# An encoder trunk on eight cores: convolutions moved up in the tail of the convolution layer, norm factors kept in PSUM, MLP roots set apart, half-precision sums moved to GpSimd

## The chip, the cores and the metric

The kernel runs on the eight cores of one Trainium2 chip, two sequences of the batch on each core; no core talks to another. The metric is the device time in microseconds (us) of the slowest core. Cores 0 to 3 form one die, 4 to 7 the other. In some executions the cores of one die, or of both, show a lower granted TensorE clock and the time is some per cent longer (in the profiled run of before die 1 had 0.815 and 5282.6 us, die 0 0.992 and 4483.3); those runs are called slow and are not compared with fast ones.

Engines: PE is TensorE, DVE is VectorE, ACT is ScalarE, POOL is GpSimd, SP is SyncE, which here only issues DMAs. In the lines of the profile nearly all work appears under the line of a helper: L334 is the matmul, L348 the activation, L351 an operation on two tensors, L355 tensor with scalar, L359 scalar-tensor-tensor, L366 a copy or cast, L372 a DMA. `arena` is the one large SBUF tile and `ps` is PSUM.

Because runs disturbed by the clock are frequent, I use two more numbers beside the official ratio. The first is the mean span of all *undisturbed cores* of a kernel: cores whose granted clock in that run was at least 0.9905, over all its runs. The second is the time of each *part* (a mixer layer or an MLP) in the profiled run, from its first matmul to the first matmul of the next part, as the mean of those undisturbed cores whose trace has all 22,320 matmuls.

## The reference, cut to what matters

Batch 16, 2048 positions, 1024 channels, four layers; each layer is a mixer and an MLP, both on an RMS-normed input and added to the residual.

```python
def conv_module(h, w_in, dw, dw_bias, ln_g, ln_b, w_out):
    val, gate = jnp.split(h @ w_in, 2, axis=-1)
    v = val * jax.nn.sigmoid(gate)
    v = depthwise_conv(v, dw, width=31, centred) + dw_bias      # shortened
    vn = (v - mean(v)) * lax.rsqrt(var(v) + LN_EPS) * ln_g + ln_b
    return jax.nn.silu(vn) @ w_out

def sq_relu_mlp(h, w_up, w_down):
    a = jax.nn.relu(h @ w_up)
    return (a * a) @ w_down

mixers = (pool, conv, fourier, pool)      # layers 0..3
for i in range(4):
    x = x + mixers[i](rms_norm(x, norm_mix[i]))
    x = x + sq_relu_mlp(rms_norm(x, norm_mlp[i]), mlp_up[i], mlp_down[i])
return rms_norm(x, final_norm)
```

## The kernel before

Each core keeps the residual of one sequence, and cuts it into four tiles `j` of 512 positions and eight chunks `c` of 128 channels. The large products use a seven-product (Strassen-like) scheme, so "H sums" and "weight sums" are additions that must be made ahead of the MLP's matmuls.

In the convolution layer, `glu(c, j)` makes v, which is written to HBM and read again in four shifted copies (`vread`); `conv(k)` convolves one chunk of one tile on TensorE, in the order of tiles 0, 1, 3, 2. For tiles 3 and 2 the sums for the LayerNorm are made by TensorE too (`flush`), into the two banks S1 and S2.

```python
def vread(k):                       # reread, one per 32 rows; ... cut
    for sh in range(4):
        self.dma("sp", ..., vslot(k)[32 * sh:32 * sh + 32], src, reads=toks)

def conv(k):
    c, j = order[k]                                   # tiles 0, 1, 3, 2
    for m in range(8):
        for q in range(4):
            self.mm(bank[32 * q:32 * q + 32, :], dg(c)[:, q * 8 + m, :], v[:, q, m:m + TT], m == 0, m == 7, skip=True)
    # ... result to C with its bias; sq = its square; cb = a bf16 copy (VectorE)
    if j > 1:
        self.copy(cb, C)
        flush(keep=1)
        late.append((j, c, cb, sq))

def flush(only=None, keep=0):
    while len(late) > keep and (only is None or late[0][0] == only):
        _, c, cb, sq = late.pop(0)
        self.mm(S1, self.cm("ones", 128), cb, c == 0, c == DC - 1)
        self.mm(S2, self.cm("ones", 128), sq, c == 0, c == DC - 1)

def ln_stats(j):                    # two reads of the banks on ScalarE, then Ln and Exp
    ...
    self.act(msq, b1, AF.Square)
    self.copy(m, b1, eng="act")
    self.tt(r, b2, msq, ALU.subtract)
    self.act(r, r, AF.Ln, ...); self.act(r, r, AF.Exp, scale=-0.5)

def ln(j, c, lag=2):                # subtract; two steps later multiply, then SiLU on ScalarE
    self.tt(C, C, M[slot[j]], ALU.subtract, eng="pool" if c % 2 or j == 2 else "dve")
    ...

# the tail
for c in range(DC):
    glu(c, 3)
    if c < 4:
        out(0, 2 * c); out(0, 2 * c + 1)
    else:
        self.sq_flush()
    if c > 0:
        conv(7 + c)
    # ...
conv(15)
for c in range(DC):
    conv(16 + c)                    # tile 3
    ln_stats(1) if c == 0 else ln(1, c - 1)
for c in range(DC):
    conv(24 + c)                    # tile 2
    # ... end of LN(1), ln_stats(3) at c == 1, then ln(3, c - 2)
    if c % 2:
        out(1, c // 2)
# ... out(1, 4..7) with ln(3); out(3, 0..7) with ln(2) and the first H sums; out(2, 0..7) with the other H sums
```

`out(j, oc)` is one chunk of the output projection of tile j; it needs all eight SiLU results of that tile. After `out(2, ·)` the MLP begins; it needs the H sums and the weight sums.

In the middle of each MLP two reciprocal roots (`hs[0]`, `hs[1]`: a matmul with ones, then Ln and Exp on ScalarE) stand 0.1 unit apart in the schedule. In the Fourier tail the pieces of H multiply x with a factor that lies in SBUF (`self.RS`).

## Time and profile before

The three runs took 4494.46 to 4496.15 us. The profiled execution had die 1 slow, so I read die 0, and of it core 1. From the list of cores (core, span, granted clock):

```profile
core 1: 4482.6 us, clock 0.992
core 4: 5283.5 us, clock 0.816
```

TensorE is busy 97% of the span. What can be won is the time in which it waits. This is the view of waits of TensorE in core 1: the engine and line that waited, the engine or DMA it waited for, then us in total, times, longest.

```profile
PE ps L334 <- ACT arena L348: 48.4, 51, 2.5
PE ps L334 <- DVE arena L351: 33.9, 27, 3.3
PE ps L334 <- DMA arena<-l_pool_w_in: 16.0, 3, 13.2
PE ps L334 <- DMA arena<-scr_mlp: 5.0, 2, 3.0
PE ps L334 <- ACT ps L348: 4.6, 7, 1.2
PE ps L334 <- DMA arena<-scr_v: 1.7, 2, 1.4
PE ps L334 <- DVE arena L366: 1.6, 4, 1.0
```

Much of it stands in the tail of the two convolution layers. The timeline of core 1 (start, length, engine, line, operation, tiles, shapes, count, and in brackets the idle time before and what ended it) shows the first chunk of out(3) of sequence 0, which goes one matmul at a time because each SiLU comes late:

```profile
773.20 0.38 PE L334 MATMUL ps<-arena 128*128 128x512 bf16 x1 [1.24 <-ACT arena L348]
...
775.28 0.38 PE L334 MATMUL ps<-arena 128*128 128x512 bf16 x1 [0.99 <-ACT arena L348]
776.95 3.22 PE L334 MATMUL ps<-arena 128*128 128x512 bf16 x8 [1.29 <-ACT arena L348]
```

A longer wait can cost more than itself. This is the wait at out(0) in this layer:

```profile
660.29 11.98 PE L334 MATMUL ps<-arena 128*128 128x512 bf16 x58 [2.47 <-ACT arena L348]
```

The granted clock in this trace (the PEclk column of a view of windows) is 0.50 from 660.22 to 663.63.

In the Fourier tail VectorE is the busy engine (35.64 of the 37.00 us from 1300 to 1337 in core 1). These are two stretches of its pieces of H in the timeline of core 1, one before and one while GpSimd adds:

```profile
1304.67 1.41 DVE L359 SCALAR_TENSOR_TENSOR arena<-arena 128x512 bf16<-128x512 f32 x2
1307.73 8.97 DVE L359 SCALAR_TENSOR_TENSOR arena<-arena 128x512 bf16<-128x512 f32 x8
1309.96 4.64 POOL L351 TENSOR_TENSOR arena<-arena 128x512 bf16<-128x512 bf16 x3 [39.30 <-DVE arena L359]
1319.30 3.14 PE L334 MATMUL ps<-arena 128*128 128x512 bf16 x7 [2.44 <-DVE arena L351]
```

Alone, two pieces take 1.41 us; of the next eight, the last four overlap GpSimd and take 1.64 us each, and TensorE waits 2.44 us at the even outputs behind them.

### The profile page before, as it was taken

The numbers are of one execution on the slowest core, as the hardware profiler recorded it, in microseconds if no ns is written. First come the engines' busy times: TensorE is split into PE (matmuls) and PEld (weight loads), VectorE is DVE, ScalarE is ACT, GpSimd is POOL, SyncE is SP. The second block draws the span as 40 slices with busy tenths as digits, with TensorE's granted clock in tenths as the row PEclk, the third lists the DMA queues.
The fourth block names the chain that finished last, engine by engine and source line by source line (L and its number), as shares of the span: only waits on it lengthen the run. The fifth ranks groups of instructions, "written<-read, shape, count | busy, mean of one in ns | idle before, by whom it ended". The sixth has DMA issues, their size and how long they took to land.

```text
span 5291.8 us, 67459 instructions; the slowest of 8 cores (4481.3 to 5291.8 us)
## 1 busy us (share of the span) xinstructions
PE 5210.3 (98%) x22320; PEld 2167.1 (41%) x22320; DVE 2788.4 (53%) x5056; ACT 2048.3 (39%) x3452; POOL 162.2 (3%) x211
## 2 busy tenths in 40 slices
PE   7999999999999999999999999999999999999998
PEld 3444433444444444444444444334444444444443
DVE  3675545665666742666535545354545645425544
ACT  4333435343434434433443334353433333343333
POOL 0000001000010000000000000010000000000000
PEclk9888887888888888888888888888888888888887
DMA  6355634455535552355822334343333133312342
GB/s 142 92 141 168 152 85 103 115 147 157 168 80 141 158 158 77 81 142 173 223 96 98 126 126 115 88 119 112 126 126 122 70 126 126 128 45 98 126 152 107
DMA packets 122742, 652.33 MB, mean 123 GB/s; under 512 B 14624, under 2 KB 55712, under 8 KB 75552
## 3 DMA queue, kind: packets, MB, share of 16 engines
q1 hardware_dynamic: 102240, 517.46, 27.5%
q0 software_dynamic: 20160, 130.56, 13.8%
q8 instruction: 185, 3.03, 0.2%
q14 instruction: 157, 1.29, 0.1%
HBM read 625.35 MB, written 151.07 MB: 147 GB/s over the span
## 4 chain that ended last, share of the span: by engine, by line
PE 95%; DVE 2%; ACT 1%; issue 1%; DMA 1%; POOL 0%; DVEq 0%; SPq 0%; ACTq 0%; POOLq 0%
PE ps L334 95%; DVE arena L351 1%; ACT arena L348 1%; DVE arena L359 1%; DMA arena<-l_pool_w_in 0%; DMA arena<-xT 0%; POOL arena L372 0%; ACT ps L348 0%; DVEq L285 0%; SPq L372 0%; ACT L348 0%; ACTq L285 0%; DVEq L1848 0%; DVE arena L355 0%; SPq L285 0%
## 5 line engine op out<-in xcount | busy, mean ns | idle before, releaser
L334 PE MATMUL ps<-arena 128*128 128x512 bf16 (+4 forms) x22320 | 5210.3, 423 | 63.5 <-ACT arena L348 28.9
L334 PEld LDWEIGHTS ps<-arena 128*128 128x128 bf16 (+1 forms) x22320 | 2167.1, 108 | 3106.1 <-issue 3002.1
L351 DVE TENSOR_TENSOR arena<-arena,ps 128x512 f32<-128x512 f32 (+2 forms) x1026 | 724.1, 718 | 1189.8 <-PE ps L334 1186.4
L351 DVE TENSOR_TENSOR arena<-arena 128x512 bf16<-128x512 bf16 (+4 forms) x2318 | 1105.9, 495 | 182.1 <-ACT arena L348 143.9
L348 ACT ACTIVATE arena<-arena 128x512 bf16<-128x512 f32 (+4 forms) x1239 | 793.6, 651 | 653.6 <-DVE arena L351 620.8
L348 ACT ACTIVATE ps<-ps 128x512 f32<-128x512 f32 x770 | 448.1, 582 | 1478.3 <-PE ps L334 1423.4
L348 ACT ACTIVATE arena<-ps 128x512 f32<-128x512 f32 (+2 forms) x1114 | 637.8, 597 | 756.2 <-PE ps L334 716.8
L351 DVE TENSOR_TENSOR arena<-ps,arena 128x512 f32<-128x512 f32 x520 | 359.4, 691 | 787.0 <-PE ps L334 735.6
L359 DVE SCALAR_TENSOR_TENSOR arena<-arena 128x512 bf16<-128x512 f32 (+1 forms) x944 | 667.2, 721 | 116.6 <-ACT arena L348 109.3
L348 ACT ACTIVATE arena<-ps,arena 128x512 bf16<-128x512 f32 (+2 forms) x294 | 185.1, 665 | 304.8 <-PE ps L334 290.2
L359 DVE SCALAR_TENSOR_TENSOR arena<-arena,ps 128x512 bf16<-128x512 f32 (+1 forms) x75 | 51.3, 695 | 139.9 <-PE ps L334 124.0
L351 POOL TENSOR_TENSOR arena<-arena 128x512 f32<-128x512 f32 (+1 forms) x61 | 83.1, 1388 | 1133.4 <-ACT arena L348 980.7
L372 POOL DMA_DIRECT2D arena<-l_mlp x96 | 50.8, 529 | 2032.9 <-PE ps L334 1474.6
L355 DVE TENSOR_SCALAR arena<-arena 128x512 bf16<-128x512 f32 (+1 forms) x112 | 46.5, 462 | 37.3 <-DMA arena<-xT 37.3
L348 ACT ACT_TABLE_LOAD x33 | 42.3, 1283 | 38.3 <-DMA arena<-xT 15.1
L366 DVE CAST arena<-arena 128x512 bf16<-128x512 f32 x32 | 20.2, 631 | 30.9 <-ACT arena L348 29.2
L372 POOL DMA_DIRECT2D arena<-l_conv_w_in x16 | 8.5, 531 | 715.3 <-DVE arena L351 611.6
L369 POOL MEMSET arena<- 128x1024 bf16 (+1 forms) x6 | 4.1, 721 | 558.8 <-PE ps L334 558.8
L372 POOL DMA_DIRECT2D arena<-l_pool_w_in x14 | 7.6, 560 | 424.9 <-PE ps L334 423.9
L355 DVE TENSOR_SCALAR arena<-ps,arena 128x512 f32<-128x512 f32 x16 | 11.9, 746 | 2.4 <-PE ps L334 2.4
L366 DVE COPY arena<-arena 128x8 bf16<-128x8 bf16 (+1 forms) x10 | 4.4, 440 | 8.6 <-ACT arena L348 8.4
L372 POOL DMA_DIRECT2D arena<-l_conv_w_out x4 | 2.1, 528 | 156.6 <-PE ps L334 156.6
(10 smaller groups left out, 7.8 us busy)
## 6 DMA issues: line engine op xcount, KB each, us to landing
arena<-scr_mlp SPq DMA_DIRECT2D x160, 1792.0 KB, 7.4
scr_mlp<-arena SPq DMA_DIRECT2D x64, 1792.0 KB, 6.0
arena<-l_mlp POOLq DMA_DIRECT2D x96, 1024.0 KB, 8.2
arena<-scr_v SPq DMA_DIRECT2D x256, 130.0 KB, 3.2
arena<-xT SPq DMA_DIRECT2D x32, 512.0 KB, 7.8
outT<-arena SPq DMA_DIRECT2D x12, 1024.0 KB, 5.1
arena<-l_conv_w_in POOLq DMA_DIRECT2D x16, 512.0 KB, 8.1
scr_v<-arena SPq DMA_DIRECT2D x64, 128.0 KB, 1.9
```

The costliest lines, as they stand in the source:

```text
L334: self.P.add("pe", lambda e: e.matmul(out, lhsT, rhs, start=start, stop=stop, skip_group_check=skip), reads=[lhsT, rhs], writes=[out])
L348: self.P.add("act", lambda e: e.activation(out, in_, func, **kw), reads=reads, writes=[out])
L351: self.P.add(eng, lambda e: e.tensor_tensor(out, in0, in1, op), reads=[in0, in1], writes=[out])
L355: self.P.add(eng, lambda e: e.tensor_scalar(out, in0, s1, None, op0), reads=reads, writes=[out])
L359: self.P.add(eng, lambda e: e.scalar_tensor_tensor(out, in0, scalar, in1, op0, op1), reads=reads, writes=[out])
L366: self.P.add(eng, lambda e: e.tensor_copy(out, in_), reads=[in_], writes=[out])
L369: self.P.add(eng, lambda e: e.memset(ap, val), writes=[ap])
L372: return self.P.add(q, lambda e: e.dma_start(out=out, in_=in_), reads=[in_] + list(reads), writes=[out] + list(writes), chan=chan, group=g ...
```

## The change

Its intent: take TensorE's waits out of the joints between the parts. In the convolution tail the convolutions of tiles 1 and 3 are issued earlier, between the GLUs, so that each LayerNorm has more matmuls to hide behind; the factors of tile 2 and of the MLP's roots stay in PSUM; the last H sums are spread differently and the four weight sums of the MLP's first slot go to GpSimd. The odd LayerNorm subtractions of tiles 0, 1 and 3 move from GpSimd to VectorE, 12 in each layer. The two roots in the MLP are set 2.2 units apart (a unit is four matmuls, 0.86 us). The Fourier tail keeps its factors in PSUM and gives more H sums to GpSimd. Pool layer 0 of the first sequence collects six banks before it needs the root. The x of the next sequence is reloaded later.

The core of the diff (cuts marked with ...):

```diff
-        eng = "dve"
+        eng = "pool" if i == 0 and KINDS[li] == "conv" else "dve"      # the MLP's weight sums
...
-        at(d0 + 3.1, hs[1])
+        at(d0 + 5.2, hs[1])                                            # the second root in the MLP
...
-                    at(14 * (NSLOT + 4 + 2 * k) + 3 + 3.3 * c, self.final_chunk, nxt, j, c, self.RS[0])
+                    at(14 * (NSLOT + 4 + 2 * k) + 3 + 3.3 * c, self.final_chunk, nxt, j, c, self.RS[0], True)
+                if nxt.after is not None:
+                    at(14 * (NSLOT + 8) + 4 + 26 * k, self.load_next, nxt, j)      # x reload, later
...
+                if k < (5 if s == 0 and li == 0 else 3):               # pool layer: collect banks
+                    continue
...
-                self.tt(C, C, M[slot[j]], ALU.subtract, eng="pool" if c % 2 or j == 2 else "dve")
+                self.tt(C, C, M[slot[j]], ALU.subtract, eng="pool" if j == 2 else "dve")
...
         for c in range(DC):                                            # convolution tail
             glu(c, 3)
-            if c < 4:
-                out(0, 2 * c)
-                out(0, 2 * c + 1)
-            ...
-            if c > 0:
-                conv(7 + c)
+            for k in {0: (8,), 4: (15,)}.get(c, (2 * c + 7, 2 * c + 8)):
+                conv(k)
+            if 1 <= c <= 4:
+                out(0, 2 * c - 2)
+                out(0, 2 * c - 1)
+            ...
+            elif c == 5:
                 self.sq_flush()
                 ln_stats(1)
+            elif c > 5:
+                ln(1, 2 * c - 12)
+                ln(1, 2 * c - 11)
+        conv(23)
+        ln(1, 4)
+        ln(1, 5)
         for c in range(DC):
             conv(24 + c)
             if c == 0:
-                ln(1, DC - 1)
-                ln(1, DC)
-            elif c == 1:
+                for k in (6, 7, DC):
+                    ln(1, k)
                 ln_stats(3)
-            else:
-                ln(3, c - 2)
-            if c % 2:
-                out(1, c // 2)
+            for k in {2: (0, 1), 3: (2,), 4: (3, 4), 5: (5,), 6: (6, 7), 7: (DC,)}.get(c, ()):
+                ln(3, k)
+            if c in (3, 5):
+                out(1, (c - 3) // 2)
+        ln_stats(2)
...
-        self.h_open(nx, (2, 3))                                        # Fourier tail
+        self.h_open(nx, (0, 1, 2), (S1, S2))
...
-                for b, r in ((S1, self.RS[0]), (S2, self.RS[1])):
-                    self.act(r, b, AF.Ln, bias=self.vcol("eps", 0))
-                    self.act(r, r, AF.Exp, scale=-0.5)
+                for b in (S1, S2):
+                    self.act(b, b, AF.Ln, bias=self.vcol("eps", 0))
+                    self.act(b, b, AF.Exp, scale=-0.5)
```

## The prediction

33, 12, 7, 3.5 and 3 us are 58.5, of which the text says 58. That a piece stays near 0.75 us with its factor in PSUM was the author's estimate; what the trace of before shows of it is seven other scalar-tensor-tensor operations (128x512, f32 output) with one input in PSUM, at 0.74 to 0.75 us each while GpSimd adds (4464.44 to 4471.1, core 1).

> **What bounds it now.** TensorE. In the list of cores, die 0 ran at a clock of 0.992 and 4481 to 4485 us; die 1 is in the slow state, so I read core 1 of die 0. In its view of waits, TensorE waits 48.4 us for ScalarE results, 33.9 for VectorE, 16.0 for the first weights, 5.0 for reloads of MLP weights, 8.9 for others: about 111 us of 4483. That can be won, plus slow restarts: after 2.5 us idle the next dozen matmuls start every 0.43 us, not 0.216 (timeline). [...] No matmul is added or removed, so the ceiling is near 2.5%.
>
> **The parts, by core 1's timeline (stall plus slow restart).**
>
> 1. Conv tail, two layers. Lost now: first out-projection 5.0 and 5.4 us, waits in the convs of tiles 3 and 2 about 3.6 and 4.0, start of out(3) 5.8 and 7.8, of out(2) 4.5 and 2.9, start of the MLP 3.1 and 5.5: 47 us. Convs moved up give the LayerNorm a lead of several PE groups, so the three out-projection stalls (31 us) should nearly vanish. The MLP start lags because VectorE owes some 20 us of work in 14 us of matmuls; the change moves 8 H sums and four MLP weight sums (0.69 us each) to GpSimd: half gained. New wait: conv 23 now follows its GLU after only two convs (4.6 us), while v's write and reread take about 6 us (landings 2.3 and 3.5): 1 to 2 us lost per layer. Gain 33 us.
> 2. MLP roots 2.2 units apart. All eight MLPs stall 1.5 to 1.8 us between the roots on one bank; 2.2 units are 1.9 us of matmuls. Gain 12.
> 3. Fourier tail, two layers, 8 us each lost (waits of 2.4, 1.5, 1.2, 0.6, and 2.5, 3.0). There VectorE is 96% busy. While GpSimd works, a piece with two SBUF inputs takes 1.64 us, not 0.75. [...] With the factor in PSUM pieces should stay near 0.75 (4 x 0.9 us saved), and four more sums leave VectorE (1.7). The wait in the even outputs goes; the MLP start's stays in part. Gain 7.
> 4. Pool layer 0: stage_in waits 2.65 and 1.0 us for the square sums; two more banks (3.45 us of matmuls) cover it. Gain 3.5.
> 5. Later x reload: core 1 loses 3.8 and 3.2 us waiting for MLP weights behind it; core 0 only 0.6. Gain for the slowest core 3.
>
> Sum 58; minus some for stalls that move: about 50.
>
> **Prediction: 4445 us, 8 in 10 between 4422 and 4468.** Faster by over 2%: 3%; within 2%: 96%; slower by over 2%: 1%.
>
> **Right if the profile shows:** TensorE's waits for ScalarE fall from 48 to about 20 us and for VectorE from 34 to about 15; no wait over 1 us at out(3) and out(2); roots without the 1.5 us stall; Fourier pieces at 0.75 us while GpSimd runs; no wait for the MLP reload near the end of sequence 0.
>
> **Wrong if:** GpSimd's sums (1.2 to 1.7 us each, 8 to 12 in a row) become the last to arrive at an MLP start; [...] PSUM factor banks held until the last piece delay outputs or the MLP; the moved convs wait longer for v's reread.

## The result, and the profile after

The fast runs of the changed kernel took 4470.15 and 4473.17 us (two more were slow: 4571.54 and 5188.51). The ratio of fast runs is 0.9948, with a 95% interval of 0.9924 to 0.9972: about 23 us faster, within 2%. Ratios in this document are the mean time of one kernel's fast runs over that of the other's in the same rounds, so they are not quite the ratio of the medians that I quote. The forecast was 4445 us with 4422 to 4468 as its range: the direction was right, and the gain was under half of what was forecast.

The profiled run was fast on all cores. In the list of cores:

```profile
core 1: 4455.9 us, clock 0.993
core 6: 4468.6 us, clock 0.992
```

TensorE's waits in core 1, the same view as before:

```profile
PE ps L334 <- ACT arena L348: 25.4, 27, 4.6
PE ps L334 <- DVE arena L351: 23.7, 25, 2.3
PE ps L334 <- DMA arena<-l_pool_w_in: 17.9, 4, 13.2
PE ps L334 <- ACT ps L348: 13.9, 15, 2.1
PE ps L334 <- DVE arena L366: 7.8, 4, 3.0
PE ps L334 <- DMA arena<-scr_v: 7.3, 4, 3.4
```

The two large lines fell by 23.0 and 10.2 us, and the wait for `scr_mlp` (5.0) is gone. But three lines that were small have grown: ScalarE's writes to PSUM by 9.3, VectorE's casts (L366) by 6.2, the reread of v by 5.6. Of 38 us taken away, 21 came back under other names.

By parts, as means of the undisturbed cores with full traces (three before, six after), in us:

| part | before | after | change | forecast |
|---|---|---|---|---|
| 2 convolution layers with the MLPs behind them | 518.8 + 796.7 | 514.1 + 794.2 | -7.2 | -33, and -3 for roots |
| 2 Fourier layers with the MLPs behind them | 235.1 + 784.7 | 223.6 + 791.6 | -4.6 | -7, and -3 for roots |
| 4 pool layers | 535.1 | 533.9 | -1.2 | -3.5 |
| MLP 3 of sequence 0, with the reload | 402.1 | 396.1 | -6.0 | -3, and -1.5 for roots |
| the 3 other MLPs | 1196.6 | 1194.5 | -2.1 | -4.5 for roots |
| sum | 4469.1 | 4448.0 | -21.1 | -58.5 |

So 28.8 of the 37.4 us by which the sum missed its forecast sit in the first row, the convolution tail. There the timeline of core 1, sequence 0, shows what answers to the lines of before. The out-projections of all four tiles no longer wait for their first operands; in their place stand these waits (the one at 782.45 is a square sum of out(3)):

```profile
725.54 2.46 PE L334 MATMUL ps<-arena 128*32 128x512 bf16 x34 [3.41 <-DMA arena<-scr_v]
739.12 6.08 PE L334 MATMUL ps<-arena 128*128 128x512 bf16 x42 [3.83 <-ACT arena L348]
757.64 0.59 PE L334 MATMUL ps<-arena 128*128 128x512 bf16 x2 [0.71 <-DVE arena L366]
761.24 4.97 PE L334 MATMUL ps<-arena 128*128 128x512 bf16 x15 [3.00 <-DVE arena L366]
782.45 7.71 PE L334 MATMUL ps<-arena 128*128 128x512 bf16 x35 [1.35 <-ACT arena L348]
808.70 3.79 PE L334 MATMUL ps<-arena 128*128 128x512 bf16 x9 [2.35 <-DVE arena L351]
```

Adding all waits of TensorE over 0.25 us in one convolution layer (core 1) gives 12.1 us before and 12.8 after in sequence 0, and 13.3 before and 12.4 after in sequence 1; with the first 10 us of the MLPs behind, 31.2 us became 29.7. This sum, "waits of the conv tails" from here on, is what the experiments act on. It differs from core to core of one run: over the undisturbed cores with full traces it is 30.7 to 34.6 before (mean 32.2) and 28.1 to 33.2 after (mean 30.9), so a difference of 2 or 3 us in core 1 alone says little. It leaves out the slow restarts: after the 3.00 us wait at 761.24 the next seven matmuls start 0.38 to 0.43 us apart, not 0.216. These did not go away either: by the trace's record of the granted clock, TensorE ran at half clock for 23.9 us of the two convolution layers before, and for 20.5 to 27.3 us after. So neither the waits nor the half-clock stretches explain the few us that the layers did gain; in core 1 about 3.5 us of it, by an estimate from the starts of the matmuls, come from there being fewer waits: a matmul of 512 columns just ahead of a wait counts 0.38 us instead of 0.216, and there are 29 of these before and 8 after.

What each new wait waits for can be followed in the same timeline.

- *Conv 23, 3.41 us.* It needs v of the last GLU. The write of v was issued at 718.27, and the rereads follow at 720.21; TensorE had only two convolutions (4.8 us with their sums) to do after the GLU's last matmul (717.34 to 722.13). In the view of DMA issues of this stretch (window from 717 to 727) each part takes, from issue to landing:

```profile
arena<-scr_v SPq DMA_DIRECT2D x12, 130.0 KB, 3.5
scr_v<-arena SPq DMA_DIRECT2D x1, 128.0 KB, 1.8
```

- *The sums of conv 26, 3.83 us.* Tiles 3 and 2 share the banks S1 and S2, so the first sum of tile 2 must wait until ScalarE has read the sums of tile 3. ScalarE reads them at 737.92, behind four SiLU of tile 1 (the first alone, then three in one line):

```profile
734.58 0.81 ACT L348 ACTIVATE arena<-arena 128x512 bf16<-128x512 f32 x1 [1.25 <-DVE arena L351]
735.79 2.22 ACT L348 ACTIVATE arena<-arena 128x512 bf16<-128x512 f32 x3 [0.39 <-DVE arena L351]
737.92 1.05 ACT L348 ACTIVATE arena<-ps 128x512 f32<-128x512 f32 x2
```

- *The last sums of tile 2, 3.00 us.* They wait for VectorE's bf16 copy of conv 31, which stands behind LayerNorm steps of tile 3 in VectorE's queue (four of them, 2.49 us, from 757.41).

In the MLPs the wait of 1.46 to 1.66 us between the roots gave way to one of 0.88 us at the next product bank. These are the two waits of MLP 2 of sequence 0 before, then after; the second is no new one, it fell from 1.16 to 0.78 us:

```profile
1484.17 7.28 PE L334 MATMUL ps<-arena 128*128 128x512 bf16 x33 [1.47 <-ACT arena L348]
1492.62 1.67 PE L334 MATMUL ps<-arena 128*128 128x512 bf16 x7 [1.16 <-DVE arena L351]
```

```profile
1479.97 3.61 PE L334 MATMUL ps<-arena 128*128 128x512 bf16 x16 [0.88 <-ACT ps L348]
1484.36 1.89 PE L334 MATMUL ps<-arena 128*128 128x512 bf16 x8 [0.78 <-DVE arena L351]
```

In the Fourier tail the pieces stay short while GpSimd adds: seven pieces in 4.69 us (started 0.66 us apart), while GpSimd works on the first of nine sums. The wait of 2.44 us at the even outputs is gone, but TensorE waits more at the start of the MLP:

```profile
1299.40 4.69 DVE L359 SCALAR_TENSOR_TENSOR arena<-arena,ps 128x512 bf16<-128x512 f32 x7
1299.51 10.80 POOL L351 TENSOR_TENSOR arena<-arena 128x512 bf16<-128x512 bf16 x9 [0.20 <-DVE arena L359]
1323.18 1.02 PE L334 MATMUL ps<-arena 128*128 128x512 bf16 x4 [1.74 <-DVE arena L351]
1326.31 2.29 PE L334 MATMUL ps<-arena 128*128 128x512 bf16 x8 [2.11 <-ACT ps L348]
```

### The profile page after: what moved, and what is told of

Its sections match the earlier page's. It is cut to its first block, busy times and chain, and to the rows that moved or that the text cites. A ratio compares the mean times of both kernels' runs of the same rounds, so it can differ in the third digit from the quotient of the medians.

```text
span 4468.6 us, 67390 instructions; the slowest of 8 cores (4451.0 to 4468.6 us)
## 1 busy us (share of the span) xinstructions
PE 4340.4 (97%) x22320; PEld 1959.7 (44%) x22320; DVE 2743.0 (61%) x5052; ACT 2017.1 (45%) x3452; POOL 159.2 (4%) x215
## 3 DMA queue, kind: packets, MB, share of 16 engines
q1 hardware_dynamic: 102240, 517.46, 33.4%
q14 instruction: 158, 1.29, 0.1%
## 4 chain that ended last, share of the span: by engine, by line
PE 88%; DVE 4%; ACT 2%; issue 2%; DMA 2%; SPq 0%; DVEq 0%; POOL 0%; ACTq 0%; POOLq 0%
PE ps L334 88%; DVE arena L351 3%; ACT arena L348 2%; DVE arena L359 1%; DMA scr_v<-arena 1%; DMA arena<-l_pool_w_in 1%; DMA arena<-l_mlp 0%; DMA arena<-scr_v 0%; SPq L372 0%; DMA arena<-xT 0%; ACT L348 0%; ACT ps L348 0%; DVE arena L355 0%; DVEq L285 0%; POOL arena L372 0%
## 5 line engine op out<-in xcount | busy, mean ns | idle before, releaser
L334 PE MATMUL ps<-arena 128*128 128x512 bf16 (+4 forms) x22320 | 4340.4, 371 | 109.9 <-ACT arena L348 25.5
L334 PEld LDWEIGHTS ps<-arena 128*128 128x128 bf16 (+1 forms) x22320 | 1959.7, 98 | 2490.0 <-issue 265.0
L351 DVE TENSOR_TENSOR arena<-arena 128x512 bf16<-128x512 bf16 (+4 forms) x2298 | 1090.3, 494 | 159.5 <-ACT arena L348 121.4
L348 ACT ACTIVATE arena<-arena 128x512 bf16<-128x512 f32 (+2 forms) x1227 | 787.8, 653 | 555.0 <-DVE arena L351 501.6
L348 ACT ACTIVATE arena<-ps 128x512 f32<-128x512 f32 (+2 forms) x1114 | 613.9, 598 | 530.9 <-PE ps L334 489.0
L359 DVE SCALAR_TENSOR_TENSOR arena<-arena 128x512 bf16<-128x512 f32 (+1 forms) x880 | 614.7, 711 | 78.6 <-ACT arena L348 71.2
L359 DVE SCALAR_TENSOR_TENSOR arena<-arena,ps 128x512 bf16<-128x512 f32 (+1 forms) x139 | 95.1, 717 | 118.9 <-PE ps L334 65.4
L351 POOL TENSOR_TENSOR arena<-arena 128x512 bf16<-128x512 bf16 (+2 forms) x65 | 80.2, 1255 | 886.9 <-ACT arena L348 732.7
L366 DVE CAST arena<-arena 128x512 bf16<-128x512 f32 x32 | 13.7, 427 | 28.8 <-ACT arena L348 27.2
L366 DVE COPY arena<-arena 128x8 bf16<-128x8 bf16 (+1 forms) x10 | 4.2, 416 | 5.1 <-ACT arena L348 4.8
## 6 DMA issues: line engine op xcount, KB each, us to landing
arena<-l_mlp POOLq DMA_DIRECT2D x96, 1024.0 KB, 10.2
```

What stands on the lines that cost most here:

```text
L334: self.P.add("pe", lambda e: e.matmul(out, lhsT, rhs, start=start, stop=stop, skip_group_check=skip), reads=[lhsT, rhs], writes=[out])
L348: self.P.add("act", lambda e: e.activation(out, in_, func, **kw), reads=reads, writes=[out])
L351: self.P.add(eng, lambda e: e.tensor_tensor(out, in0, in1, op), reads=[in0, in1], writes=[out])
L359: self.P.add(eng, lambda e: e.scalar_tensor_tensor(out, in0, scalar, in1, op0, op1), reads=reads, writes=[out])
L366: self.P.add(eng, lambda e: e.tensor_copy(out, in_), reads=[in_], writes=[out])
```

## The experiments

Two theories of the convolution tail were open. The *order theory*: the stalls come from what stands ahead of the needed result in ScalarE's and VectorE's queues; a better order removes them. The *throughput theory*: ScalarE and VectorE have about as much work in the tail as TensorE, so a wait that is taken out at one joint comes back at the next, and only less work helps. Eleven kernels were run, in three groups, each group on one chip and beside runs of the kernel before. The changed kernel (after) has runs of its own only from the first comparison, none in these groups. All gave correct results.

Columns: ratio of fast runs to the fast runs of before of the same group, with its interval; mean span of undisturbed cores (their number); waits of the conv tails in core 1, in us (for h_sums_early core 5, as die 0 was disturbed); the two convolution layers in us, and the sum of all parts.

| kernel | ratio of fast runs | undisturbed cores | conv waits | conv layers | all parts |
|---|---|---|---|---|---|
| before | 1 | 4486.0 (43), 4485.1 (37), 4484.9 (49) in the three groups | 31.2 | 518.8 | 4469.1 |
| after | 0.9948 [0.9924, 0.9972] | 4464.9 (21) | 29.7 | 514.1 | 4448.0 |
| e1 conv alone | 0.9966 [0.9927, 1.0006] | 4474.8 (28) | 28.8 | 513.9 | 4462.4 |
| e2 all but conv | none: one fast run, 4510.79 | 4471.2 (18) | 35.7 | 523.4 | 4457.4 |
| e3 GLU ahead | 0.9968 [0.9912, 1.0024] | 4458.6 (31) | 32.2 | 511.0 | 4444.9 |
| e4 statistics first | 0.9968 [0.9915, 1.0021] | 4461.1 (20) | 30.3 | 512.3 | 4449.4 |
| e5 LN(3) later | 1.0025 [0.9932, 1.0118] | 4460.6 (16) | 29.7 | 514.1 | 4446.1 |
| e6 subtractions on GpSimd | none: one fast run, 4465.42 | 4454.0 (18) | 27.0 | 508.7 | 4443.6 |
| e7 second root later | 0.9955 [0.9869, 1.0040] | 4459.5 (18) | 29.5 | 515.2 | 4447.4 |
| e8 H sums early | 0.9941 [0.9863, 1.0020] | 4460.0 (26) | 31.0 | 514.8 | 4444.1 |
| e9 reordered tail | 0.9947 [0.9892, 1.0002] | 4449.4 (26) | 24.1 | 501.4 | 4436.6 |
| e10 reordered tail, with e6, e7, e8 | 0.9850 [0.9789, 0.9911] | 4437.4 (32) | 19.5 | 498.5 | 4426.3 |
| e11 e6, e7, e8 without the new tail | 0.9884 [0.9794, 0.9974] | 4447.9 (26) | 25.9 | 507.2 | 4435.7 |

The intervals of the official ratios are wide because many runs that count as fast still had a die at a clock of 0.98. I therefore rest small differences on the last three columns, and take nothing under about 3 us in the convolution layers, or 5 us between means of undisturbed cores (their standard deviation is 4 to 6 us), as a finding. The column of all parts is coarser: single cores of the changed kernel lie between 4437.8 and 4454.3. The wait for the first weights alone moves it by several us: pool layer 0 of sequence 0 took from 144.0 to 152.4 us over the cores of these runs, with the same code from e3 to e11 and in the kernel after.

### e1 and e2: the convolution tail alone, and everything but it

Kept of the change in e1, on the kernel before: the new order of convs, GLUs, LayerNorm steps and out-projections; the factors in PSUM there; the H and weight sums moved to GpSimd there. In e2: the rest (roots, Fourier tail, pool layer, reload).

```diff
 # e1, against before                         # e2, against before
+for k in {0: (8,), 4: (15,)}.get(...)        +at(d0 + 5.2, hs[1])
+    conv(k)                                  +self.h_open(nx, (0, 1, 2), (S1, S2))
+m, r = M[slot[j]], S2 if j == 2 else ...     +at(14 * (NSLOT + 8) + 4 + 26 * k, self.load_next, nxt, j)
```

> The kernel before with only the conv tail part of the change. Theory M (the conv stalls moved rather than went): from the two traces the conv layers plus the MLPs behind them lost 77 us of TensorE time before and 68 us after, so the conv part alone gains 6 to 12 us, far under the 33 forecast. Rival C (the conv part is worth its 30 us, and the other parts cost something): gains 25 us or more.

> The changed kernel with the conv tail part undone. Theory M: gains 12 to 20 us over the kernel before (roots 4, Fourier 5, pool layer 2 to 4, reload 0 to 7 by core). Rival C: gains nothing or loses. Together with the run of the conv part alone the gains should add up to about the 23 us of the whole change; if not, the parts interact.

Measured: undisturbed cores end 11.2 us earlier than before with the tail alone and 14.8 us earlier with the rest; the whole change gives about 21, less than the 26 of the two. (By the sums of parts it is 6.7 and 11.7 against 21.1, so the two measures do not agree on an interplay.) Both runs fall within what theory M expected, and e1 is far from rival C's 25. In the parts the tail alone takes 4.9 us off the convolution layers and 1.5 off the MLPs behind them. Its new waits are those of the whole change, to a few tenths (3.41, 3.83 and 3.00 there; here the first and the last of the three, the middle one is 3.61):

```profile
729.81 11.64 PE L334 MATMUL ps<-arena 128*32 128x512 bf16 x134 [3.56 <-DMA arena<-scr_v]
...
767.11 19.60 PE L334 MATMUL ps<-arena 128*128 128x512 bf16 x84 [3.00 <-DVE arena L366]
```

What follows: the gain that is missing is lost inside the tail, not mainly by the interplay of the parts. The tail's new order by itself trades its old waits (31.2 us) for new ones (28.8). In e2 the old waits are all there (35.7), and the convolution layers took 523.4 us, 4.6 more than before with the same code in the tail; why stays open (two waits of 1.77 and 1.24 us for the reread of v in core 1 are part of it). No run of e2 but one was fast, so it has no ratio.

### e3, e4, e5: one new wait each, by order

Each takes aim at one of the three new waits, by position in the queues alone.

```diff
 # e3: convs of tile 3 spread over the last GLUs, statistics of tile 1 later
-            for k in {0: (8,), 4: (15,)}.get(c, (2 * c + 7, 2 * c + 8)):
+            for k in {0: (8,), 4: (15,), 5: (17,), 6: (18,), 7: (19, 20)}.get(c, (2 * c + 7, 2 * c + 8)):
...
+            elif c == 6:
                 ln_stats(1)
...
 # e4: statistics of tile 3 ahead of the rest of LN(1)
             if c == 0:
+                ln_stats(3)
                 for k in (6, 7, DC):
                     ln(1, k)
-                ln_stats(3)
...
 # e5: the last steps of LN(3) behind out(1, 2)
-            for k in {2: (0, 1), 3: (2,), 4: (3, 4), 5: (5,), 6: (6, 7), 7: (DC,)}.get(c, ()):
+            for k in {2: (0, 1), 3: (2,), 4: (3, 4), 5: (5,), 6: (6,)}.get(c, ()):
...
+            if oc == 2:
+                ln(3, 7)
+                ln(3, DC)
```

> The changed kernel with the last three GLUs of tile 3 put two convs earlier, so that four convs (9 us of matmuls) instead of two lie between the last GLU and conv 23. Theory M1: the 3.4 us wait of conv 23 for the reread of v from DRAM is due to its distance alone and vanishes (under 0.5 us), worth 3 to 4 us in each of two layers, 6 to 8 in all. Rival T (VectorE and ScalarE are simply full in this stretch, so any wait taken away returns as another): the time stays within 2 us of the changed kernel.

> The changed kernel with the statistics of tile 3 put ahead of the last LayerNorm steps of tile 1 instead of behind them, nothing else. Theory M2: the 3.8 us wait in conv 26 is the sum banks of tile 3 still being unread, because their readers queue behind four SiLU evaluations (0.8 us each) on ScalarE; it falls under 1.5 us, and the half-rate convs after it (1 us) go too: 3 to 4.5 us in each of two layers. Rival T: another wait of the same size appears within the next ten us, time within 2 us of the changed kernel.

> The changed kernel with the last LayerNorm steps of tile 3 (chunk 7 and the flush of the lag) moved from before to after the statistics of tile 2. Theory M3: the 3.0 us wait of the last sum matmuls for a VectorE cast is the cast of conv 31 queued behind those LayerNorm steps; it falls under 2 us, and the half-rate restart after it (1.2 us) with it: 2 to 4 us in each of two layers. Rival T (VectorE is full there): the wait returns at the next out-projection of tile 1 or at out(3), time within 2 us of the changed kernel.

Measured, in core 1, sequence 0. With the GLU ahead (e3) the wait at conv 23 fell from 3.41 to 2.44 us only, and 1.60 us appeared at conv 31. Its GLU's tanh now stood on ScalarE behind the Ln and Exp of tile 1 with two table loads of 1.28 us, and ran at 719.70; so TensorE had 4.7 us more of convolutions to do, but the write of v went out 3.0 us later (721.29). With the statistics first (e4) the 3.83 us at the sums of conv 26 became two waits of 2.21 and 2.41 us at the sums of conv 27 (for VectorE's copy, then for ScalarE). Conv 23 waited a microsecond longer (4.46 us), ahead of the edit: this wait varies from 3.23 to 4.46 us in core 1 of the runs that share its code. With LN(3) later (e5) the 3.00 us at the last sums became 1.80, and the square sum in out(3) waited 3.15 instead of 1.35. One line of each shows the wait that was left or had moved:

```profile
729.28 2.47 PE L334 MATMUL ps<-arena 128*32 128x512 bf16 x34 [2.44 <-DMA arena<-scr_v]
```

```profile
745.98 15.47 PE L334 MATMUL ps<-arena 128*128 128x512 bf16 x155 [2.41 <-ACT arena L348]
```

```profile
781.22 8.97 PE L334 MATMUL ps<-arena 128*128 128x512 bf16 x33 [3.15 <-ACT arena L348]
```

What follows: the waits of the conv tails stayed at 29.7 to 32.2 us, against 29.7 (29.0 to 30.4 against 30.9 in the mean of the cores). Each aimed-at wait did shrink, but only e5's came down as far as its expectation said. M1 was wrong that distance alone decides: the tanh had moved too. M2's wait split in two instead of falling under 1.5 us. One position changed at a time mostly moves a wait. Up to here the throughput theory had the better of it. (The convolution layers of e3 were 3.1 us shorter in the mean of three cores, the one small gain among the three. e5's ratio above 1 comes from runs with die 1 at a clock of 0.986; its undisturbed cores are no slower.)

### e6: less work on VectorE

The change had moved the odd LayerNorm subtractions of tiles 0, 1 and 3 back from GpSimd to VectorE. This run puts them on GpSimd again, 12 in each layer.

```diff
-                self.tt(C, C, M[slot[j]], ALU.subtract, eng="pool" if j == 2 else "dve")
+                self.tt(C, C, M[slot[j]], ALU.subtract, eng="pool" if c % 2 or j == 2 else "dve")
```

> The changed kernel with the odd LayerNorm subtractions back on GpSimd (12 per layer, 0.69 us each on VectorE), as before the change. Rival T (the moved stalls are VectorE's load): the waits in the convs of tiles 3 and 2 shrink by about half and the kernel gains 6 us or more. Theory M (they are the order in which results are asked for): two of the three waits do not start with VectorE, so they stay within 1 us; and VectorE instructions with two SBUF inputs stretch beside GpSimd (from 0.69 to 1.2 to 1.8 us, as in the trace before), so the gain is under 3 us or a loss.

Measured: the two convolution layers 508.7 us against 514.1, the waits 27.0 against 29.7 (27.1 against 30.9 in the mean of the cores), undisturbed cores 4454.0 against 4464.9. Of these 10.9 us some 4 are no gain of this edit: e5 of the same group, with convolution layers as long as after's, stood at 4460.6. The two waits on VectorE's copy (0.71 and 3.00) became one of 2.40; those at conv 23 and conv 26 stayed at 3.23 and 3.69:

```profile
760.50 19.75 PE L334 MATMUL ps<-arena 128*128 128x512 bf16 x84 [2.40 <-DVE arena L366]
```

What follows: VectorE's load does carry part of the tail, worth about 5.5 us (rival T asked for 6 or more, theory M for under 3), and one line of the change itself had gone the wrong way. Most of the waits are untouched by it, so load is not the whole cause.

### e7 and e8: the roots, and the H sums of the Fourier tail

```diff
 # e7
-        at(d0 + 5.2, hs[1])
+        at(d0 + 6.1, hs[1])
 # e8: the last four H sums ahead of the last even output, not behind the first odd one
+            if k == 3:
+                for q in range(4, 8):
+                    h[26 + q]()
             out_pair(1, k, 0, (1, 0, 3, 1)[k])
```

> The changed kernel with the second MLP root after, not before, the ScalarE copy at unit 6 of the same group. Theory R: the 0.9 us that remain of the root stall are this copy queued behind the second root's Ln and Exp on ScalarE; in sequence 1 the wait falls from 0.9 to under 0.5 us in each of four MLPs, in sequence 0 it partly reappears at the VectorE wait 4 us later: 1 to 3 us in all. Rival B (the wait is still the one bank that both roots use): the wait stays at 0.9 us.

> The changed kernel with the last four H sums on VectorE (0.42 us each) moved from between the odd outputs to before the adds of the last even output, where VectorE idles 0.9 and 1.3 us. Theory F: the wait at the MLP start behind the Fourier layer (1.7 and 2.1 us) is VectorE's queue of output adds, 1.7 us longer for these four sums; it falls by 1.5 us in each of two layers, 3 us in all. Rival G (the wait is GpSimd's twelve sums arriving last): no change.

Measured, e7: TensorE's wait for ScalarE's copy to PSUM in this part is gone (the total of that line fell from 13.9 to 6.6 us in core 1), but in sequence 0 the wait on VectorE about 4 us later grew from 0.78 to 1.69 us (in sequence 1, 0.31 to 0.37 us is left there):

```profile
1485.39 4.91 PE L334 MATMUL ps<-arena 128*128 128x512 bf16 x22 [1.69 <-DVE arena L351]
```

The three MLPs with no other change (MLP 0 of both sequences and MLP 3 of sequence 1) took 1192.9 us together against 1194.5. That would be another 0.5 us per MLP. It is below what I count in a single run, but e10 and e11 came to 1192.8 as well. ScalarE's copy was what the wait was for, as theory R had it; in sequence 0 the wait has moved on to VectorE.

Measured, e8: the MLPs behind the Fourier layers took 786.9 us, against 791.6 after, and the Fourier layers 223.1 against 223.6. The first wait of that MLP shrank from 1.74 to 0.31 us; the second, for ScalarE, stayed (2.06, in core 5):

```profile
1325.20 1.07 PE L334 MATMUL ps<-arena 128*128 128x512 bf16 x4 [0.31 <-DVE arena L351]
...
```

What follows: part of what the Fourier tail gained was given back at the start of the MLP because four H sums were queued on VectorE behind the outputs. Moving them gives back about 5 us over two layers, more than the 3 that theory F expected, and rival G (no change) is out.

### e9, e10, e11: the whole tail reordered, and everything together

If single moves only shift a wait, all have to be made at once. e9 does the same work as the changed kernel in another order throughout the tail:

```diff
-                flush(keep=1)
+                flush(keep=2)                      # sums may lag two convs
...
-                sq3_add(2)
+                sq3_add(3)
...
-            for k in {0: (8,), 4: (15,)}.get(c, (2 * c + 7, 2 * c + 8)):
+            for k in {0: (8,), 4: (15,), 5: (17,), 6: (18,), 7: (19,)}.get(c, (2 * c + 7, 2 * c + 8)):
                 conv(k)
...
-        conv(23)
-        ln(1, 4)
-        ln(1, 5)
+        ln_stats(1)                                # after the last GLU
+        for k, lns in ((20, ()), (21, ()), (22, (0,)), (23, (1,))):
+            conv(k)
+            for q in lns:
+                ln(1, q)
...
+        # steps after conv 24 + c: s = statistics, o = a chunk of out(1), else ln(j, q)
+        plan3 = {0: [(3, 's'), (1, 2), (1, 3), (1, 4), (1, 5)], 1: [(1, 6), (1, 7)], 2: [(1, 8)], 3: [(3, 0), (3, 1)],
+                 4: [], 5: [(0, 'o')], 6: [(3, 2)], 7: [(3, 3), (3, 4), (0, 'o')]}
...
+        # steps after out(1, oc)
+        tail = {2: [(3, 5)], 3: [], 4: [(3, 6), (3, 7), (2, 0), (2, 1), (2, 2), (2, 3), (2, 4)], 5: [(3, 8)], 6: [], 7: []}
... (and the MLP's first root after LN(2) instead of during it)
```

e10 is e9 with the edits of e6, e7 and e8; e11 is the changed kernel with those three and the old tail.

> The same work as the changed kernel, only in another order in the tail of both conv layers: the convs of tile 3 are spread over the last three GLUs, the statistics of tile 1 come after the last GLU, those of tile 3 directly after the first conv of tile 2, the square sums may lag two convs, the norm steps of tile 3 go mostly behind the out-projection of tile 1, the root for the MLP behind the norm of tile 2. Order theory (the stalls come from what stands ahead in ScalarE's and VectorE's queues): no single TensorE wait over 2 us is left in the conv tail, each conv layer falls from 257 to 240 to 246 us with the MLP behind it no longer, undisturbed cores end at 4430 to 4445 us. Throughput theory (ScalarE and VectorE have more work than TensorE's time in the tail, whatever the order): the waits move to the out-projections and the MLP start, conv layer and MLP together shorten by under 3 us each, undisturbed cores stay above 4457 us.

> The run before this one, and with it the three small parts that were tried alone: every odd subtraction of the norm on GpSimd, the second MLP root 0.9 unit later, the H sums of the Fourier tail ahead of the last even output. If the stalls of the tail, of the roots and of the Fourier layer's MLP start are independent of each other, the gains add: another 4 to 5 us at the two Fourier MLPs, 2 to 3 at the roots, 0 to 5 in the conv tails (less than the 5.5 it gave alone, as the order has by then hidden part of VectorE's time), undisturbed cores at 4420 to 4435 us. If they share one limit, under 4 us beyond the run before this one.

> The same three small parts on the changed kernel without the reordered tail. Alone they took 5.5, 2.5 and 4.5 us out of the parts they aim at. If independent: undisturbed cores near 4452 us, 12 us under the changed kernel, with the waits at conv 23 (3 to 4 us) and at the square sums in conv 26 (3.7) unchanged. If not: 4457 or above.

Measured, e9: the convolution layers fell from 514.1 to 501.4 us and the MLPs behind them stayed (794.8 against 794.2); the waits fell from 29.7 to 24.1 (from 30.9 to 23.1 in the mean of the cores), and the time at half clock in these layers from 20.5 to 27.3 us to 13.7 to 17.1. In sequence 0 no wait at conv 23 is left, and the longest at the sums is 1.16 us; conv 31 waits 1.57 us for its reread. But a wait has come back where the kernel before had it, at the first chunk of out(3), one SiLU at a time:

```profile
772.39 0.38 PE L334 MATMUL ps<-arena 128*128 128x512 bf16 x1 [2.96 <-ACT arena L348]
...
776.59 19.38 PE L334 MATMUL ps<-arena 128*128 128x512 bf16 x81 [1.94 <-ACT arena L348]
```

The layers came to 251.7 and 249.7 us, from 257.2 and 257.0, and undisturbed cores to 4449.4. That lies between the two forecasts: the order is worth 12.8 us over the two layers, far more than the throughput theory allowed, and about half of what the order theory asked for.

Measured, e10: on top of e9 the convolution layers lose 2.8 us, the MLPs behind the Fourier layers 5.4, the other three MLPs 1.9; undisturbed cores end at 4437.4, 12.0 us under e9 (a little later than forecast) and 47.5 under before. The waits at out(3) shrink to 0.89, 1.29 and 1.29 us. Its fast runs took 4443.71 to 4471.70 us, at a ratio of 0.985 to before, with an interval of 0.9789 to 0.9911: faster for certain, but whether by 2% is unclear. The ratio flatters it, as some of before's fast runs in this group were disturbed (up to 4547.57 us); the 47.5 us between undisturbed cores are 1.1%. It beats both kernels, though it was not run beside the changed one: its parts sum to 21.7 us less. TensorE's waits in core 1:

```profile
PE ps L334 <- DVE arena L351: 27.6, 30, 2.5
PE ps L334 <- ACT arena L348: 22.4, 30, 1.6
...
```

Measured, e11: the sum of parts is 4435.7 (two cores), that is 12.3 us under the changed kernel, and the new waits of the tail are still there (4.00 us at conv 23, 3.69 at conv 26).

What follows: e9 (11.4 us less than after, in the sum of parts) and e11 (12.3 less) nearly add up in e10 (21.7 less of 23.7). The three small parts and the order are mostly separate causes; in the convolution layers e6 and e9 may share something, as the load is worth 5.5 us without the new order and 2.8 with it, a difference at the limit of what I count.

A likely reason that order could not do it all is in a view of windows. These are the last stretch of the tail, from the first matmul of out(3) to the MLP, in core 1 of before and of e9, with the stretch, its length, then busy us (and instructions) of PE, weight load, DVE, ACT and POOL, clock, DMA share and GB/s:

```profile
770.93:810.88 39.95, 33.71 (x139) 14.06 (x138) 33.40 (x53) 21.48 (x28) 9.11 (x7) 0.91 0.15 27
```

```profile
767.71:806.97 39.26, 32.32 (x138) 13.78 (x137) 34.52 (x47) 17.85 (x25) 20.61 (x13) 0.91 0.00 1
```

VectorE is busy 33.4 of 39.95 us before and 34.5 of 39.3 in e9 (84% and 88%), as much as TensorE before and more in e9. In e10, with the subtractions on GpSimd, the stretch took 37.05 us with VectorE busy 31.1. In the changed kernel, whose waits stand earlier, it took 31.1 us with VectorE busy 24.4 (78%); over its whole tail (697.47 to 804.68) VectorE is busy 66.3 of 107.2 us, and ScalarE 60.3. So there is room earlier and little at the end of e9's order. That this is what stops a better order was not tested by itself.

## Why the prediction was wrong

The step that failed is in part 1, the convolution tail: "Convs moved up give the LayerNorm a lead of several PE groups, so the three out-projection stalls (31 us) should nearly vanish." The three stalls did vanish. The error was to book their whole length as gain. The waits of the conv tails went from 31.2 to 29.7 us (32.2 to 30.9 in the mean of the cores), the time at half clock in these layers did not fall (23.9 us before, 20.5 to 27.3 after), and the two convolution layers with their MLPs gained 7.2 us, not 33. Moving TensorE's work ahead left ScalarE and VectorE their work in nearly the same order, with 12 subtractions a layer added to VectorE, so TensorE met late results at three other places: the reread of v at conv 23, which the moved convolutions brought on themselves, the first sums of tile 2, and its last sums. Single reorderings (e3 to e5) left the sum at 29.7 to 32.2; taking those subtractions off VectorE (e6) won 5.5 us; a new order throughout (e9) won 12.8.

Point by point:

- *"New wait: conv 23 ... 1 to 2 us lost per layer."* Foreseen, and too small: 3.41 us at conv 23 and 0.47 at the next one in sequence 0, 0.67 at conv 22 and 2.77 at conv 23 in sequence 1. I had added a landing of 2.3 us for the write and of 3.5 for the reads. In the trace 0.9 us pass from the GLU's last matmul (717.34) to the write, which landed after 1.8; the four rereads are issued one after the other over 2.2 us, so 5.2 us pass from the first issue to the last landing (725.41). That makes 8.1 us, against 4.8 us of matmuls.
- *The waits on the shared sum banks and on the bf16 copy.* Not seen at all. They were no waits of the kernel before, and I had costed only those that the old profile showed.
- *"The MLP start ... half gained."* In part: 5.9 us of waits in the first 10 us of the two MLPs became 4.5.
- *"MLP roots ... Gain 12."* The mechanism was right, the size was not. The wait on one bank between the roots is gone, but the second root's Ln and Exp now delay ScalarE's copy of a product bank (e7 shows it), and 0.88 us of about 1.5 came back. The three MLPs with no other change gained 2.1 us, 0.7 each; 1.5 each had been forecast. Another 0.9 unit (e7) adds about 0.5.
- *"Fourier tail ... Gain 7."* The cause was right: with the factor in PSUM a piece stays at 0.74 us beside GpSimd (16 of them in core 1 of after), against 1.64 with both inputs in SBUF (4 in core 1 of before). The layers gained 11.5 us and the MLPs behind them lost 6.9, net 4.6. Of those 6.9, in core 1, 4.6 only cross the line between the parts: before, the waits of 1.54 and 3.02 us stood ahead of the MLP's first matmul, now the waits stand ahead of its fifth. e8 won 4.7 us there by queueing four sums earlier.
- *"Pool layer 0 ... Gain 3.5"* and *"Later x reload ... Gain 3."* Small and of the right sign: 1.7 us in pool layer 0 of sequence 0 (149.4 to 147.7), within what the first weights' arrival moves, though the two waits of 2.65 and 1.00 us for the square sums are gone in core 1; MLP 3 of sequence 0 gained 6.0 on the mean of cores, and TensorE's waits for `scr_mlp` (5.0 us in core 1) are gone.
- *"waits for ScalarE fall from 48 to about 20 us and for VectorE from 34 to about 15."* 25.4 and 23.7; and 21 us came back under three lines I had not put a number on. Of "no wait over 1 us at out(3) and out(2)" one failed: the square sum in out(3) waits 1.35 us.
- *"Sum 58; minus some for stalls that move: about 50."* I knew that stalls move and took off 8 us for it. In the convolution tail nearly all of it moved.

What stays open: why the mean spans of e3, e4, e5 and e7 are 4 to 6 us under that of the changed kernel, when their sums of parts are between 3.1 under and 1.5 over it. I have no runs of the changed kernel in those groups, so it may be the chip or the hour; I don't rest anything on it, and the spans of e6 and of e9 to e11 set against that of the changed kernel carry the same doubt.

## What to carry to other kernels

A wait that the profile shows at one joint is worth its length only if the engine that made it late gets ahead of the next joint too: before booking the gain, redo the queues of the helper engines for the new order and look for the next result that comes late. Where one engine's queue is the cause, move all the joints at once (e9: 12.8 us off the convolution layers) and take work off that engine (e6: 5.5 us); a single move mostly carries the wait along (e3 to e5: waits of 29.7 to 32.2 us, against 29.7). When something is offloaded to make room (here H sums to GpSimd), check that the same change does not put other work back (here the 12 subtractions a layer).

## What the traces show of the hardware

- In core 1 of before a wait of 2.47 us was followed by seven matmuls 0.38 to 0.70 us apart, and in core 1 of after one of 3.00 us by seven at 0.38 to 0.43; while after 2.99 us at 2197.46 of before, and after 3.41 us at conv 23 of after, the matmuls ran at their usual pace (the first 32 of conv 23, four in about 0.21 us). The stretches at half clock mostly last 3.41 us (13 of 15 in core 1 of before, 10 of 12 in core 1 of after). So the length of a wait alone did not decide; what did was not shown.
- A table load on ScalarE took 1.28 us. No further time is seen around it: in e3 a load began at 718.40, 0.02 us after the activations before it ended, and the tanh behind it began at 719.70, again 0.02 us after the load, so a switch cost 1.3 us. In core 1 of the changed kernel ScalarE's next operation begins 0.01 us after the load in all 33 cases.
- A scalar-tensor-tensor piece of 128x512 with two SBUF inputs took 0.75 us alone and 1.64 us beside GpSimd's sums. The sums took 1.35 to 1.60 us each beside such pieces, and 1.15 us beside pieces with their factor in PSUM. Casts of 128x512 (f32 to bf16, their one input in SBUF) took 0.43 us alone; of the three that lie wholly beside GpSimd's sums in core 1 of before, two took 1.46 and 1.48 us.
- From the issue of a 128 KB write to HBM (718.27) to the landing of the last of four rereads of 130 KB of the same data (725.41) 7.1 us passed. The write took 1.8 us to land, the rereads 2.7 to 3.6 each; they were issued one after the other over 2.2 us.
